# Experts in an order found on the chip: many and few tokens in turn, weights addressed by register

## The chip, the core and the metric

The kernel runs on one core of one Trainium2 chip, in one launch. The metric is the device time of that core in microseconds (us), from the first to the last instruction with what lies around it; lower is better. An expert's weights are 12 MiB of float32 (8 MiB for the gate and up projection, 4 MiB for the down projection), and all 32 experts are read from the chip's memory once: 384 MiB.

## The reference, cut to what matters

One layer of a diffusion block runs over 256 latent tokens of width 1024. Its first half (adaLN, a Fourier branch, a gated linear recurrence, a merge) is not touched by the change. Its second half is a mixture of 32 experts, of which each token takes the four with the highest router logits:

```python
logits = (t @ w_router + b_router).astype(jnp.float32)
top_v, top_i = lax.top_k(logits, TOP_K)          # 4 of 32
wts = jax.nn.softmax(top_v, axis=-1)
...
gu = xb @ w_gu[e] + b_gu[e]                      # (n, 1024) @ (1024, 2048)
gate = jnp.minimum(gu[:, :D_EXPERT], SWIGLU_LIMIT)
up = jnp.clip(gu[:, D_EXPERT:], -SWIGLU_LIMIT, SWIGLU_LIMIT)
act = (up + 1.0) * gate * jax.nn.sigmoid(SWIGLU_ALPHA * gate)
yb = act @ w_down[e] + b_down[e]                 # (n, 1024) @ (1024, 1024)
```

The result of each expert is weighted with `wts` and added into its tokens' rows; a gated residual add and a final norm follow. How many tokens an expert has depends on the data. Worked out from the reference with its inputs, the counts of experts 0 to 31 are 19, 63, 12, 15, 42, 19, 53, 12, 22, 7, 17, 49, 20, 38, 25, 54, 40, 32, 26, 81, 78, 35, 23, 65, 77, 18, 18, 35, 6, 7, 9, 7.

## The kernel before

The first half of the program, some 330 us, is written by a planner (lines 106 to 1018). It ends with the router. What matters here is the loop over the experts (line 1364).

**Weights.** SyncE issues every load of weights, in the order of the list `todo` (lines 188 to 198): gu0, gu1, dn0, gu2, dn1, gu3, dn2 and so on. `gu{e}.{k}` are the eight loads of 1 MiB of an expert's gate and up weights, `dn{e}.{k}` the four of its down weights. Every load needs one of 19 slots (`NSLOT`, line 46). `drop` gives a slot back, `pump` issues the next load into it; in the program a load then waits for the last reader of the slot that it takes. For experts 0 and 1 a slot comes free as each step k ends (line 1334). For the others all eight `gu` slots are dropped behind the conditional blocks (line 1344), and so are the four `dn` slots (line 1422). Besides, a load waits for the load eight before it to land.

**Routing.** Lines 1030 to 1050 make the logits, their mask `msk`, the place `pos` of each token in its expert's list, and the counts. `pick` and `gather` (lines 1058 and 1069) collect the rows of two experts by a matmul with a one-hot matrix. The counts are loaded into registers of TensorE, ScalarE and VectorE (line 1222); on TensorE this load stands between the first gather and the first expert.

**Experts 0 and 1** are computed with 64 rows each (`gate_up`, line 1094). **Each other expert** has room for 32 rows in one pass: `up32` (line 1111) multiplies 32 rows with all eight `gu` tiles; with more than 32 tokens a second pass runs under a condition on the count (line 1340), with more than 64 a third (line 1342). `swiglu` follows each pass. `turn` (line 1348) transposes the result, and `down` (line 1141) multiplies with the four `dn` tiles, again under the two conditions (lines 1417 and 1419; the third pass is `third_down`, line 1297). TensorE's order in an iteration e is: up of expert e + 1, a gather for the next two experts if e is even, `add_rows` (line 1283) in every fourth iteration, down of expert e, turn of expert e + 1. The experts run in the order of their index, whatever their counts are. With the counts above, experts 19, 20, 23 and 24 need three passes, experts 4, 6, 11, 13, 15, 16, 21 and 27 two, and the other 18 of the 30 one.

Of the kernel before, what the change touches and what calls it, by code (L numbers as in the profile page):

```python
# [32 lines left out]
D = 1024  # L33
# [46 lines left out]

S_C, S_CC, S_N1, S_N2, S_CW, S_CB, S_GA, S_GX, S_LAM, S_END = 0, 8, 16, 24, 32, 64, 72, 88, 104, 120

C_ID, C_UT, C_IO, C_END = 0, 128, 256, 512

B_CH, B_END = 512, 768

# [4 lines left out]
def block_kernel(ctx: ExitStack, tc: tile.TileContext, x, cx, small, b_ada, w_ada0, w_ada, w_in, gate_w,  # L91
# [84 lines left out]
    for it, j in seq:  # L176
# [8 lines left out]
        elif it[0] == "ada":  # L185
            todo.append((f"ada{8 + c}", w_ada[c // 8, c % 8], 1))

    for e in range(NE + 1):
        if e < NE:
            for k in range(KD):  # L190
                todo.append((f"gu{e}.{k}", w_gu[e * D + k * P:e * D + (k + 1) * P], 1))
        if e:
            d = e - 1
            for k in range(KD // 2):
                todo.append((f"dn{d}.{k}", w_dn[d * FE + 2 * k * P:d * FE + 2 * (k + 1) * P].rearrange(
                    "(a p) f -> p a f", p=P), 2))
            if d == 3:
                todo.append(("bd", b_dn, 0))
# [832 lines left out]
    rs2 = rstd_of(sq, 2)  # L1031
    for j in range(2):
        ada_row(ada_b[2], 2 + j, g2b[:, j * 512:(j + 1) * 512])
    pc, p = bank(), bank()
    for t in range(2):
        V.scalar_tensor_tensor(lg[:, t, :NE], pl[t][:, :NE], rs2[:, t:t + 1], lb, op0=OP.mult, op1=OP.add)
    for t in range(2):
# [6 lines left out]
    PE.matmul(p[:, :NE], lhsT=before, rhs=msk[:, 0], start=True, stop=True)  # L1044
    PE.matmul(p[:, NE:2 * NE], lhsT=before, rhs=msk[:, 1], start=True, stop=False)
    PE.matmul(p[:, NE:2 * NE], lhsT=ones, rhs=msk[:, 0], start=False, stop=True)
    for t in range(2):
        PE.matmul(pc[0:1, :NE], lhsT=ones[:, 0:1], rhs=msk[:, t], start=t == 0, stop=t == 1)
    V.scalar_tensor_tensor(pos, p[:, :2 * NE].rearrange("p (t e) -> p t e", t=2), 1.0, msk, op0=OP.add, op1=OP.mult)
    cnt = per.tile([1, NE], I32, name="cnt")  # L1050

    def col(a, t, e):
        return a[:, t, e:e + 1] if e != "x" else cols[:, (2 if a is wts else 0) + t:(2 if a is wts else 0) + t + 1]

    def pick(parts):

# [9 lines left out]
    def gather(gm, tiles):  # L1069

        n = gm.shape[-1]
        w = min(n, P)
        m = 4 if n <= P else 2
        per_tile = 512 // w
        xT = [tiles[k // per_tile][:, k % per_tile * w:(k % per_tile + 1) * w] for k in range(KD)]
        xM = [tiles[-1][:, k * CAP:(k + 1) * CAP] for k in range(KD)]
        ps = [bank() for _ in range(KD // m)]
        for k in range(KD):
            p = ps[k // m][:, k % m * n:(k % m + 1) * n]
            for t in range(2):  # L1080
                PE.matmul(p, lhsT=xs[:, t, k * P:(k + 1) * P], rhs=gm[:, t], start=t == 0, stop=t == 1)  # L1081
        for k in range(KD):
            p = ps[k // m][:, k % m * n:(k % m + 1) * n]
            for o, c in ((xT[k], slice(0, w)), (xM[k], slice(w, n)))[:1 if n <= P else 2]:
                if k % 2:
                    S.activation(o, p[:, c], AF.Identity, bias=mod2[:, 0, k:k + 1], scale=mod2[:, 1, k:k + 1])  # L1086
                else:
                    V.tensor_scalar(o, p[:, c], mod2[:, 1, k:k + 1], mod2[:, 0, k:k + 1], op0=OP.mult, op1=OP.add)  # L1088
        return xT, xM

    def one_of(e):
        return sel[:, e:e + 1] if e != "x" else selx

    def gate_up(e, ps, xT, ks):

# [110 lines left out]
    def add_start(bd):  # L1206
# [244 lines left out]
def _constants():  # L1451
    ca = np.zeros((P, C_END), np.float32)
    ca[:, C_ID:C_ID + P] = np.eye(P)
    ca[:, C_UT:C_UT + P] = np.triu(np.ones((P, P)), 1)
    ca[:, C_IO:C_IO + T] = np.arange(1, T + 1)[None, :]
    l, k = np.meshgrid(np.arange(T), np.arange(T), indexing="ij")
    th = 2 * np.pi * ((l * k) % T) / T
    dft = np.concatenate([np.cos(th)[:, :N_C], np.sin(th)[:, 1:T // 2]], 1).reshape(2, P, T).transpose(1, 0, 2)
    l, k = np.meshgrid(np.arange(P), np.arange(P), indexing="ij")
    th = 2 * np.pi * ((l * k) % P) / P  # L1460
    s = 1.0 / math.sqrt(T * P)
    cb = np.concatenate([dft.reshape(P, 2 * T), s * np.cos(th), -s * np.sin(th)], 1).astype(np.float32)
    return ca, cb
# [53 lines left out]
```

## Time and profile before

| what | value |
|---|---|
| runs, median (lowest to highest) | 1343.27 us (1332.36 to 1345.16), 3 runs |
| the profiled execution: its time | 1340.13 us |
| the profiled execution: its span | 1338.3 us, granted TensorE clock 0.905 of full |
| TensorE busy (matmul) | 1109.0 us, 83% |
| VectorE, ScalarE, GpSimd busy | 43%, 20%, 10% |
| DMA queue of SyncE | 86.1% of 16 engines over the span, 464.77 MB |

The profile shows one execution. Times in it count from the first instruction. PE stands for TensorE's matmuls, PEq, SPq and DVEq for the sequencers of TensorE, SyncE and VectorE. In the slices and windows PEclk is the granted TensorE clock as a share of full speed, and GB/s is what the core's 16 DMA engines moved. In a row of the timeline the first number is when the row starts, the second how long it lasts, xN how many instructions it holds, and the bracket how long the engine sat idle before and what ended that.

### The profile page before, as it was taken

What the parts mean: (1) busy time and instruction counts of PE and PEld (TensorE: products, weight loads), DVE (VectorE), ACT (ScalarE), POOL (GpSimd) and SP (SyncE); (2) the same over time, 40 slices, a digit from 0 to 9 for tenths busy, and PEclk for the clock granted to TensorE, in tenths of its full rate; (3) what the DMA queues carried; (4) which work ended last, traced back from release to release, by engine and by line L of the source; (5) the groups of instructions that cost most, each with busy time, mean ns of one, the idle gap of its engine ahead of it and who ended that gap; (6) DMA issues with size and microseconds to landing.
All of it is one profiled execution on the core that took longest, in us unless ns stands there. A gap on an engine that the chain in (4) does not pass through costs nothing. (4 is left out here: it accounts for less than half of the span.)

```text
span 1338.3 us, 22548 instructions
## 1 busy us (share of the span) xinstructions
PE 1109.0 (83%) x9393; PEld 619.1 (46%) x9393; DVE 574.2 (43%) x1131; ACT 270.7 (20%) x460; POOL 133.6 (10%) x125
## 2 busy tenths in 40 slices
PE   5998987889898787876878688769998988897765
PEld 4897875678444242423333243324443424443322
DVE  4469788975233332224233233323343424333222
ACT  4355686512211010101101010101010100110101
POOL 4237346600000000000000000000000000000000
PEclk8998988989998886879899899879998989998888
DMA  9920535479899999999999999999798959999994
GB/s 378 406 122 32 220 120 220 173 303 400 335 386 414 402 415 416 410 408 414 414 416 413 414 414 414 415 414 413 309 368 342 399 240 394 388 414 413 413 413 168
DMA packets 82617, 467.11 MB, mean 349 GB/s; under 512 B 8329, under 2 KB 8465, under 8 KB 42681
## 3 DMA queue, kind: packets, MB, share of 16 engines
q1 hardware_dynamic: 82457, 464.77, 86.1%
q8 instruction: 126, 2.06, 0.6%
q14 instruction: 34, 0.28, 0.1%
HBM read 463.69 MB, written 1.05 MB: 347 GB/s over the span
## 5 line engine op out<-in xcount | busy, mean ns | idle before, releaser
L1117 PE MATMUL bank<-slot,t2k 128*32 128x512 f32 x2944 | 378.8, 663 | 25.1 <-DMA slot<-in_w_gu 23.4
L1117 PEld LDWEIGHTS bank<-slot,t2k 128*32 128x32 f32 x2944 | 99.2, 120 | 273.0 <-issue 225.9
L1150 PE MATMUL bank<-slot,t2k 128*32 128x256 f32 (+1 forms) x3008 | 196.1, 406 | 14.4 <-issue 6.6
L1125 DVE TENSOR_SCALAR t2k<-bank 64x512 f32<-64x512 f32 (+1 forms) x36 | 24.6, 683 | 339.1 <-PE bank L1120 311.6
L242 PE MATMUL bank<-slot 128*128 128x256 f32 x512 | 152.0, 297 | 12.8 <-DVE slot L231 8.0
L244 PE MATMUL bank<-slot 128*128 128x256 f32 x512 | 149.5, 292 | 5.2 <-DVE slot L235 5.2
L1150 PEld LDWEIGHTS bank<-slot,t2k 128*32 128x32 f32 (+1 forms) x3008 | 107.4, 116 | 99.6 <-issue 42.6
L243 PE MATMUL bank<-slot 128*128 128x256 f32 x512 | 149.0, 291 | 0.7 <-DVE slot L235 0.7
L242 PEld LDWEIGHTS bank<-slot 128*128 128x128 f32 x512 | 102.5, 200 | 21.8 <-DVE slot L231 8.9
L244 PEld LDWEIGHTS bank<-slot 128*128 128x128 f32 x512 | 102.4, 200 | 6.0 <-DVE slot L235 6.0
L243 PEld LDWEIGHTS bank<-slot 128*128 128x128 f32 x512 | 102.4, 200 | 1.5 <-DVE slot L235 1.0
L1081 PE MATMUL bank<-gm,xs 128*128 128x192 f32 (+1 forms) x512 | 87.5, 330 | 15.0 <-PEq L1342 5.5
L1360 ACT ACTIVATE t2k<-bank 128x512 f32<-128x512 f32 x32 | 19.1, 597 | 395.7 <-PE bank L1359 395.7
L1081 PEld LDWEIGHTS bank<-gm,xs 128*128 128x128 f32 x512 | 82.9, 193 | 25.4 <-issue 22.7
L1126 ACT ACTIVATE t2k<-t2k 64x512 f32<-64x512 f32 (+1 forms) x36 | 22.7, 630 | 345.1 <-DVE t2k L1125 345.1
L1359 PE MATMUL bank<-ca,t2k 64*128 64x64 f32 (+1 forms) x128 | 17.4, 265 | 80.6 <-DVEq L1419 36.2
L1170 DVE TENSOR_TENSOR m<-bank,row 32x256 f32<-32x256 f32 x56 | 23.3, 417 | 128.1 <-PE bank L1150 127.7
L1170 DVE TENSOR_TENSOR b<-bank,row 32x256 f32<-32x256 f32 x112 | 47.3, 422 | 42.7 <-PE bank L1150 41.4
L235 DVE TENSOR_TENSOR slot<-slot 128x1024 fp32r<-128x1024 f32 (+1 forms) x40 | 54.1, 1362 | 15.8 <-ACT slot L228 12.9
L1359 PEld LDWEIGHTS bank<-ca,t2k 64*128 64x128 f32 (+1 forms) x128 | 12.5, 161 | 98.0 <-issue 56.4
L1086 ACT ACTIVATE t2k<-bank,mod 128x128 f32<-128x128 f32 x124 | 45.3, 429 | 60.4 <-DVE t2k L1088 60.2
L228 ACT ACTIVATE slot<-slot 128x1024 fp32r<-128x1024 f32 x39 | 40.6, 1054 | 58.1 <-PE bank L244 26.6
(281 smaller groups left out, 1144.7 us busy)
## 6 DMA issues: line engine op xcount, KB each, us to landing
slot<-in_w_gu SPq DMA_DIRECT2D x256, 1024.0 KB, 19.7
slot<-in_w_down SPq DMA_DIRECT2D x128, 1024.0 KB, 20.0
slot<-in_w_ada SPq DMA_DIRECT2D x24, 1024.0 KB, 8.9
slot<-in_w_in SPq DMA_DIRECT2D x18, 1024.0 KB, 10.0
slot<-in_w_rnn SPq DMA_DIRECT2D x4, 1024.0 KB, 5.6
slot<-in_w_out SPq DMA_DIRECT2D x4, 1024.0 KB, 7.9
slot<-in_gate_w SPq DMA_DIRECT2D x2, 1024.0 KB, 16.4
slot<-in_w_fourier SPq DMA_DIRECT2D x2, 1024.0 KB, 6.3
```

The source lines that it names most:

```text
L228: S.activation(hi, src, AF.Copy)
L235: V.tensor_sub(lo, src, hi)
L242: PE.matmul(p, lhsT=l[0], rhs=r[0], start=start, stop=False, skip_group_check=True)
L243: PE.matmul(p, lhsT=l[0], rhs=r[1], start=False, stop=False, skip_group_check=True)
L244: PE.matmul(p, lhsT=l[1], rhs=r[0], start=False, stop=stop, skip_group_check=True)
L1081: PE.matmul(p, lhsT=xs[:, t, k * P:(k + 1) * P], rhs=gm[:, t], start=t == 0, stop=t == 1)
L1086: S.activation(o, p[:, c], AF.Identity, bias=mod2[:, 0, k:k + 1], scale=mod2[:, 1, k:k + 1])
L1117: PE.matmul(p[j * SUB:(j + 1) * SUB], lhsT=xT[k], rhs=wt[:, j * 512:(j + 1) * 512], start=k == 0, stop=False, skip_group_check=True)
L1125: V.tensor_scalar(g, ps[0], LIMIT, None, op0=OP.min)
L1150: PE.matmul(p[h * n:(h + 1) * n, :w], lhsT=aT[:, o:o + n], rhs=wt[:, (k % 2) * D + h * w:(k % 2) * D + (h + 1) * w], start=k == 0, stop=k ...
L1170: V.tensor_mul(y[j // 2][o:o + SUB, j % 2 * 256:(j % 2 + 1) * 256], p[j * SUB:(j + 1) * SUB], g2b[j * SUB:(j + 1) * SUB, j * 256:(j + 1) * ...
L1359: PE.transpose(p[:, o:o + n], g[:, c * P:(c + 1) * P], ident[:n, :n])
```

## The change

Experts 0 and 1 stay where they are. For the other 30 the chip ranks the experts by their counts (ties by index), and a fixed table says which rank runs at which place: rank 2 (most tokens), rank 31 (fewest), rank 9, rank 24, rank 3, rank 30, rank 10, rank 23 and so on. With the counts above the passes at places 2 to 31 are 3 1 2 1, 3 1 2 1, 3 1 2 1, 3 1 2 1, 2 1 2 1, 2 1 1 1, 2 1 1 1, 1 1 (before: 1 1 2 1 2 1 1 1 1 2 1 2 1 2 2 1 1 3 3 2 1 3 3 1 1 2 1 1 1 1).

- `ordr` holds the counts by place (32 numbers) and the expert at each place (32 more). It is made from six small VectorE operations on [96, 32] and two small matmuls, behind the first gather.
- SyncE loads the expert of a place into a register (`values_load`, one for each of 30 places), and the 360 loads of those experts' weights take their address from it.
- `to_places` permutes `pos` and `wts` into `pw` by a matmul with the permutation, behind expert 0's up; `selp` does so for the bias rows. From place 2 on the code reads `pw` and `selp`.

```diff
+PAIRS = (0, 7, 1, 8, 2, 9, 3, 10, 4, 11, 5, 12, 6, 13, 14)
...
     def load(name, src, a):
         t = slot(name)
+        if callable(src):
+            src = src()
...
+    def expert(e):
+        if e < FIRST:
+            return e
+        if e not in places:
+            places[e] = nc.values_load(ordr[0:1, NE + e:NE + e + 1], engines=[ET.SP], min_val=0, max_val=NE - 1,
+                                       skip_runtime_bounds_check_because="the index of an expert by construction")
+        return places[e]
+
+    def rows_at(w, e, r, n):
+        return w[bass.ds(expert(e) * D + r, n)] if e >= FIRST else w[e * D + r:e * D + r + n]
...
-                todo.append((f"gu{e}.{k}", w_gu[e * D + k * P:e * D + (k + 1) * P], 1))
+                todo.append((f"gu{e}.{k}", lambda e=e, k=k: rows_at(w_gu, e, k * P, P), 1))
...
+    p96 = bank()
     for t in range(2):
-        PE.matmul(pc[0:1, :NE], lhsT=ones[:, 0:1], rhs=msk[:, t], start=t == 0, stop=t == 1)
+        PE.matmul(p96[:3 * NE, :NE], lhsT=ones[:, :3 * NE], rhs=msk[:, t], start=t == 0, stop=t == 1)
...
-    V.tensor_copy(cnt, pc[0:1, :NE])
...
+    V.scalar_tensor_tensor(junk, iota0[:3 * NE], 1.0, sel, op0=OP.mult, op1=OP.mult, accum_out=cc[:, 1:2])
+    V.tensor_add(key, p96[:3 * NE, :NE], ca[:3 * NE, C_TI:C_TI + NE])
+    V.scalar_tensor_tensor(junk, key, 1.0, sel, op0=OP.mult, op1=OP.mult, accum_out=cc[:, 2:3])
+    V.scalar_tensor_tensor(junk, key, cc[:, 2:3], ones[:3 * NE, :NE], op0=OP.is_gt, op1=OP.mult,
+                           accum_out=cc[:, 3:4])
+    V.tensor_scalar(pm, ca[:3 * NE, C_RK:C_RK + NE], cc[:, 3:4], None, op0=OP.is_equal)
+    V.scalar_tensor_tensor(junk, p96[:3 * NE, :NE], 1.0, sel, op0=OP.mult, op1=OP.mult, accum_out=cc[:, 0:1])
     xT, xM = gather(gm, [t2k(), t2k()])
+    pc = bank()
+    for i in (1, 0):
+        PE.matmul(pc[0:1, i * NE:(i + 1) * NE], lhsT=cc[:NE, i:i + 1], rhs=pm[:NE], start=True, stop=True)
+    V.tensor_copy(ordr, pc[0:1, :2 * NE])
+    V.tensor_scalar(selp, ca[:3 * NE, C_RK:C_RK + NE], cc[:, 3:4], None, op0=OP.is_equal)
+
+    def to_places():
+
+        p = bank()
+        for i, a in enumerate((pos, wts)):
+            for t in range(2):
+                PE.transpose(p[:NE, (2 * i + t) * P:(2 * i + t + 1) * P], a[:, t], ident)
+        q = t2k()[:NE]
+        V.tensor_copy(q, p[:NE])
+        p = bank()
+        for i in range(4):
+            PE.matmul(p[:, i * NE:(i + 1) * NE], lhsT=q[:, i * P:(i + 1) * P], rhs=pm[:NE], start=True, stop=True)
+        V.tensor_copy(pw, p[:, :4 * NE].rearrange("p (i e) -> p i e", i=4))
...
     up(0)
+    to_places()
     turn(0)
...
+    ca[:, C_RK:C_RK + NE] = np.array([0, 1] + [r for i in PAIRS for r in (2 + i, NE - 1 - i)])[None, :]
```

On SyncE's queue, before: the loads from expert 0 on, with fixed addresses.

```order
L152 DMA slot<-in_w_gu 128x2048 x16
L152 DMA slot<-in_w_down 128x2x1024 x4
L152 DMA slot<-in_w_gu 128x2048 x8
L152 DMA slot<-in_w_down 128x2x1024 x4
L152 DMA slot<-in_w_gu 128x2048 x4
```

The same place now; `cnt` is the tile of `ordr`, and the ISA rows work out an address in registers.

```order
L156 DMA slot<-in_w_gu 128x2048 x16
L156 DMA slot<-in_w_down 128x2x1024 x4
L200 TENSOR_LOAD cnt
L156 ISA
L156 DMA slot<-in_w_gu 128x2048
L156 ISA
L156 DMA slot<-in_w_gu 128x2048
```

One register load for each place from the third on, and one address instruction for each of its 12 loads, have come in; the order of the loads among themselves is the same, place for expert.

On TensorE, before: from the counts to expert 0's up.

```order
L1046 MATMUL bank<-msk,ones 128x32
L1048 MATMUL bank<-msk,ones 1x32 x2
L1081 MATMUL bank<-gm,xs 128x128 x16
L1222 TENSOR_LOAD cnt
L1100 MATMUL bank<-slot,t2k 64x512 x32
```

The same place now.

```order
L1065 MATMUL bank<-msk,ones 128x32
L1070 MATMUL bank<-msk,ones 96x32 x2
L1104 MATMUL bank<-gm,xs 128x128 x16
L1234 MATMUL bank<-t2k 1x32 x2
L1276 TENSOR_LOAD cnt
L1123 MATMUL bank<-slot,t2k 64x512 x32
```

The two matmuls that make `ordr` now stand between the gather and the register load. (Behind expert 0's bias matmuls, ahead of the transposes of its result, stand the eight matmuls of `to_places` too.)

On VectorE, before: between the first one-hot matrix and the evictions of the first gather.

```order
L1049 SCALAR_TENSOR_TENSOR pos<-bank,msk 128x64
L1064 TENSOR_SCALAR gm<-ca,pos,rs 128x64 x4
L1195 CAST cnt<-bank 1x32
L1088 TENSOR_SCALAR t2k<-bank,mod_156 128x128 x4
L1198 TENSOR_SCALAR ex<-v_3045 128x1
```

The same place now.

```order
L1087 TENSOR_SCALAR gm<-ca,pos,rs 128x64 x4
L1224 SCALAR_TENSOR_TENSOR t2k<-iota_165,sel 96x32
L1225 TENSOR_TENSOR t2k<-bank,ca 96x32
L1226 SCALAR_TENSOR_TENSOR t2k<-t2k,sel 96x32
L1227 SCALAR_TENSOR_TENSOR t2k<-t2k,ones 96x32
L1229 TENSOR_SCALAR t2k<-ca,t2k 96x32
L1230 SCALAR_TENSOR_TENSOR t2k<-bank,sel 96x32
L1111 TENSOR_SCALAR t2k<-bank,mod_156 128x128 x4
L1235 CAST cnt<-bank 1x64
L1236 TENSOR_SCALAR selp<-ca,t2k 96x32
L1252 TENSOR_SCALAR ex<-v_3045 128x1
```

The six ranking operations stand ahead of the evictions, and the copy that the register loads wait for has moved behind them.

## Rows read from the trace of the kernel before

**Rows 1.** The page's 40 equal slices of the span (33.5 us each).

```profile
PEclk8998988989998886879899899879998989998888
GB/s 378 406 122 32 220 120 220 173 303 400 335 386 414 402 415 416 410 408 414 414 416 413 414 414 414 415 414 413 309 368 342 399 240 394 388 414 413 413 413 168
```

**Rows 2.** Windows: us; busy (count) of each engine; PEclk, DMA share, GB/s.

```profile
440.00:940.00 500.00, 399.43 (x3506) 174.95 (x3502) 155.48 (x392) 47.10 (x103) 0.00 (x0) 0.88 1.02 413
940.00:1180.00 240.00, 211.13 (x2169) 97.60 (x2165) 92.62 (x223) 21.69 (x45) 0.00 (x0) 0.94 0.87 350
```

**Rows 3.** The costliest groups of the page: the passes of up32.

```profile
L1117 PE MATMUL bank<-slot,t2k 128*32 128x512 f32 x2944 | 378.8, 663 | 25.1 <-DMA slot<-in_w_gu 23.4
```

**Rows 4.** Who SyncE waited for, 920 to 1130 us: total, times, longest.

```profile
SPq L152 <- PE bank L1120: 49.5, 3, 26.3
SPq L152 <- PEq L1342: 32.0, 2, 17.4
```

**Rows 5.** Timeline of TensorE, 1075 to 1122 us: expert 24's up, expert 23's down.

```profile
1078.34 0.66 PE L1359 MATMUL bank<-ca,t2k 64*128 64x64 f32 x4 [2.64 <-DVEq L1419]
...
1080.91 9.04 PE L1117 MATMUL bank<-slot,t2k 128*32 128x512 f32 x64
...
1089.99 7.04 PE L1117 MATMUL bank<-slot,t2k 128*32 128x512 f32 x64
...
1097.08 7.04 PE L1117 MATMUL bank<-slot,t2k 128*32 128x512 f32 x64
...
1104.17 7.08 PE L1150 MATMUL bank<-slot,t2k 128*32 128x256 f32 x128
...
1114.12 3.66 PE L1150 MATMUL bank<-slot,t2k 128*32 128x256 f32 x64 [0.15 <-DVE t2k L1138]
1118.74 2.87 PE L1311 MATMUL bank<-t2k 32*128 32x512 f32 x8 [0.96 <-DVE t2k L1170]
1121.55 0.46 PE L1359 MATMUL bank<-ca,t2k 64*128 64x64 f32 x4
```

**Rows 6.** Timeline of SyncE over the same stretch: first issue, time over all.

```profile
1076.28 28.24 SPq L152 DMA_DIRECT2D slot<-in_w_gu  x5
```

**Rows 7.** Windows of 10 us: one in the later stall, one in the early one.

```profile
1095.00:1105.00 10.00, 10.00 (x108) 3.14 (x104) 3.35 (x5) 0.63 (x1) 0.00 (x0) 1.00 0.00 0
...
390.00:400.00 10.00, 9.05 (x68) 2.86 (x62) 3.17 (x5) 0.63 (x1) 0.00 (x0) 1.00 0.83 310
```

**Rows 8.** Timeline of TensorE, 355 to 395 us: the turn to experts 1 and 2.

```profile
357.52 0.81 PE L1359 MATMUL bank<-ca,t2k 128*128 128x128 f32 x4 [2.69 <-DVE t2k L1129]
...
387.06 7.07 PE L1117 MATMUL bank<-slot,t2k 128*32 128x512 f32 x64
```

**Rows 9.** Timeline of SyncE, from 380 us: the four issues ahead of expert 2's release.

```profile
381.44 14.02 SPq L152 DMA_DIRECT2D slot<-in_w_gu  x5
```

**Rows 10.** Register loads of lines 1222 and 1395: ns min/median/max, start.

```profile
L1222 PEldq TENSOR_LOAD <-cnt x1: 2317/2317/2317, 337.9 to 337.9; - x1
...
L1395 SPq TENSOR_LOAD <-more x1: 492/492/492, 554.9 to 554.9; - x1
```

**Rows 11.** Timeline of all engines, 336 to 358 us: the start of expert 0.

```profile
336.25 0.17 DVE L1195 CAST cnt<-bank 1x32 int32<-1x32 f32 x1
336.25 3.81 PE L1081 MATMUL bank<-gm,xs 128*128 128x128 f32 x32 [1.00 <-DVE gm L1064]
...
340.44 13.95 PE L1100 MATMUL bank<-slot,t2k 128*64 128x512 f32 x64 [0.38 <-issue]
...
341.04 0.41 DVE L1088 TENSOR_SCALAR t2k<-bank,mod 128x128 f32<-128x128 f32 x1 [0.53 <-ACT t2k L1086]
...
343.61 0.19 DVE L1200 SCALAR_TENSOR_TENSOR wts<-wts,msk 128x32 f32<-128x32 f32 x1 [2.10 <-ACT wts L1199]
...
354.65 0.69 DVE L1125 TENSOR_SCALAR t2k<-bank 128x512 f32<-128x512 f32 x1 [9.24 <-PE bank L1107]
```

**Rows 12.** Timeline of TensorE, 1059 to 1076 us: what two and four experts share.

```profile
1059.78 5.47 PE L1081 MATMUL bank<-gm,xs 128*128 128x192 f32 x32
...
1068.51 3.60 PE L1287 MATMUL bank<-b,ctx 128*128 128x512 f32 x8
```

More of the change, by code (lines that the diff above doesn't have):

```diff
@@ L81 @@
 S_C, S_CC, S_N1, S_N2, S_CW, S_CB, S_GA, S_GX, S_LAM, S_END = 0, 8, 16, 24, 32, 64, 72, 88, 104, 120
-C_ID, C_UT, C_IO, C_END = 0, 128, 256, 512
+C_ID, C_UT, C_IO, C_RK, C_TI, C_END = 0, 128, 256, 512, 544, 576
+PAIRS = (0, 7, 1, 8, 2, 9, 3, 10, 4, 11, 5, 12, 6, 13, 14)
 B_CH, B_END = 512, 768
@@ L186, in block_kernel @@
             todo.append((f"ada{8 + c}", w_ada[c // 8, c % 8], 1))
+    places = {}
+    ordr = None
+    def expert(e):
[7 more added lines that the diff above has]
+        return w[bass.ds(expert(e) * D + r, n)] if e >= FIRST else w[e * D + r:e * D + r + n]
     for e in range(NE + 1):
@@ L194, in block_kernel @@
             for k in range(KD // 2):
-                todo.append((f"dn{d}.{k}", w_dn[d * FE + 2 * k * P:d * FE + 2 * (k + 1) * P].rearrange(
+                todo.append((f"dn{d}.{k}", lambda d=d, k=k: rows_at(w_dn, d, 2 * k * P, 2 * P).rearrange(
                     "(a p) f -> p a f", p=P), 2))
@@ L1033, in block_kernel @@
         ada_row(ada_b[2], 2 + j, g2b[:, j * 512:(j + 1) * 512])
-    pc, p = bank(), bank()
+    p = bank()
     for t in range(2):
@@ L1046, in block_kernel @@
     PE.matmul(p[:, NE:2 * NE], lhsT=ones, rhs=msk[:, 0], start=False, stop=True)
+    V.scalar_tensor_tensor(pos, p[:, :2 * NE].rearrange("p (t e) -> p t e", t=2), 1.0, msk, op0=OP.add, op1=OP.mult)
+    ordr = per.tile([1, 2 * NE], I32, name="cnt")
+    p96 = bank()
     for t in range(2):
-        PE.matmul(pc[0:1, :NE], lhsT=ones[:, 0:1], rhs=msk[:, t], start=t == 0, stop=t == 1)
-    V.scalar_tensor_tensor(pos, p[:, :2 * NE].rearrange("p (t e) -> p t e", t=2), 1.0, msk, op0=OP.add, op1=OP.mult)
-    cnt = per.tile([1, NE], I32, name="cnt")
+        PE.matmul(p96[:3 * NE, :NE], lhsT=ones[:, :3 * NE], rhs=msk[:, t], start=t == 0, stop=t == 1)
     def col(a, t, e):
-        return a[:, t, e:e + 1] if e != "x" else cols[:, (2 if a is wts else 0) + t:(2 if a is wts else 0) + t + 1]
+        o = 2 if a is wts else 0
+        if e == "x":
+            return cols[:, o + t:o + t + 1]
+        return a[:, t, e:e + 1] if e < FIRST else pw[:, o + t, e:e + 1]
     def pick(parts):
@@ L1091, in one_of @@
     def one_of(e):
-        return sel[:, e:e + 1] if e != "x" else selx
+        return selp[:, e:e + 1] if e != "x" else selx
     def gate_up(e, ps, xT, ks):
@@ L1194, in block_kernel @@
     gm = pick([(0, 0, CAP), (1, 0, CAP)])
-    V.tensor_copy(cnt, pc[0:1, :NE])
-    xT, xM = gather(gm, [t2k(), t2k()])
+    pw = per.tile([P, 4, NE], F32, name="pw")
+    selp = per.tile([3 * NE, NE], BF, name="selp")
+    work = t2k()[:3 * NE]
+    key, pm, junk, cc = work[:, :NE], work[:, NE:2 * NE], work[:, 2 * NE:3 * NE], work[:, 3 * NE:3 * NE + 4]
+    V.scalar_tensor_tensor(junk, iota0[:3 * NE], 1.0, sel, op0=OP.mult, op1=OP.mult, accum_out=cc[:, 1:2])
[5 more added lines that the diff above has]
+    V.scalar_tensor_tensor(junk, p96[:3 * NE, :NE], 1.0, sel, op0=OP.mult, op1=OP.mult, accum_out=cc[:, 0:1])
+    xT, xM = gather(gm, [t2k(), t2k()])
+    pc = bank()
[10 more added lines that the diff above has]
+        V.tensor_copy(q, p[:NE])
+        p = bank()
+        for i in range(4):
+            PE.matmul(p[:, i * NE:(i + 1) * NE], lhsT=q[:, i * P:(i + 1) * P], rhs=pm[:NE], start=True, stop=True)
+        V.tensor_copy(pw, p[:, :4 * NE].rearrange("p (i e) -> p i e", i=4))
     for t in range(2):
@@ L1222, in block_kernel @@
     _, counts = nc.values_load_multi_w_load_instructions(
-        cnt, engines=[ET.PE, ET.Activation, ET.DVE],
+        ordr[0:1, :NE], engines=[ET.PE, ET.Activation, ET.DVE],
         skip_runtime_bounds_check_because="a count of tokens, from 0 to 256 by construction")
@@ L1455, in _constants @@
     ca[:, C_IO:C_IO + T] = np.arange(1, T + 1)[None, :]
+    ca[:, C_RK:C_RK + NE] = np.array([0, 1] + [r for i in PAIRS for r in (2 + i, NE - 1 - i)])[None, :]
+    ca[:, C_TI:C_TI + NE] = np.where(np.arange(NE) < FIRST, 4 * T * (FIRST - np.arange(NE)), -np.arange(NE) / NE)[None, :]
     l, k = np.meshgrid(np.arange(T), np.arange(T), indexing="ij")
```

## The prediction

> **What bounds the kernel now.** I read the 40 slices first. From the thirteenth slice on GB/s stands near 414 almost throughout: the loads of the experts' weights run at the rate that they can have, and the end comes when the last has landed. So a microsecond counts where the DMA engines move less than that. The slices show two such places behind the router: around the eleventh, and seven slices from 309 to 240 and back to 388 [rows 1]. The windows give the sizes: 413 GB/s over the 500 us from 440 to 940, and 350 over the 240 us from 940 to 1180 [rows 2]. Had the second stretch run at 413, its bytes would have taken 240 x 350/413 = 203.4 us, so 36.6 us are lost there.
>
> Why they are lost is read from the queue of SyncE. It waited there longest for the end of an expert's up, in one wait 26.3 us [rows 4]. Experts 19, 20, 23 and 24, of three passes each, lie in this stretch. The last of expert 24's passes ends some 23 us after the first began, and only then do its eight slots come free [rows 5]; five issues by SyncE take 28.24 us over them [rows 6], and from 1095 to 1105 nothing is moved while TensorE is busy all the time [rows 7]. The cause is therefore that TensorE has more to do there than the loads take, with 19 slots between them. That there are many such passes can be counted: 2944 records of up32 at 64 for a pass [rows 3, 5] are 46 passes, 16 more than the 30 experts need at least, as the counts say (4 experts with two more, 8 with one more).
>
> The balance per expert: 12 loads of 1.0486 MB at 413 GB/s take 30.5 us. A three-pass expert takes three passes of 7.04, its bias matmuls of 0.4, and a down side of 17.4 from 1104.17 to 1121.6 [rows 5]: 39.0 us. A one-pass expert takes 7.04 + 0.4 + 3.66 and some 3.3 for its turn with the 2.64 us wait before it [rows 5]: 14.4. A two-pass expert takes 14.1 + 0.4 + 7.1 + 3.3 = 24.9. Two experts share a gather of 5.47, four an `add_rows` of twice 3.6 [rows 12]. Experts 19 to 24, with 3, 3, 2, 1, 3 and 3 passes, three gathers and one `add_rows`, come to 219 us of TensorE against 183 us of loads: 36 us too much, which is what the window lost.
>
> **The change part by part.**
>
> (a) The stretch from 940 to 1180 loses its cause. In the new order a group of four places has 3, 1, 2 and 1 passes at most: 39.0 + 14.4 + 24.9 + 14.4 + 2 x 5.47 + 7.2 = 110.8 us of TensorE against 4 x 30.5 = 121.9 us of loads. On average TensorE keeps up, with 11 us to spare in a group. Gain: 36.6 us. It can't be more there; it could be less by what (e) says.
>
> (b) The start. No load is under way while expert 0 waits, as all 19 slots are full and expert 0's up must release the first, so what delays expert 0 delays the end. Before, TensorE's register load began at 337.9 beside the gather, took 2.32 us [rows 10], and expert 0 began at 340.44, 0.2 us behind it [rows 11]. Now that load waits for `ordr`, which VectorE copies behind the last eviction, begun at 341.04 and 0.41 long; with the copy's 0.17 [rows 11] that is 341.6, plus 2.32 and 0.2 is 344.1: 3.7 us later. The six ranking operations, at the 0.19 of a like one [rows 11] and some gaps under 2 us in all, lie beside the gather's 3.81 us of matmuls and are taken as hidden; if that cover fails they push the evictions by up to 1 us. Bounds 2 and 5.
>
> (c) `to_places`. Its four transposes lie in the 2.69 us in which TensorE waits for expert 0's swiglu [rows 8]. Then VectorE copies [32, 512], 0.69 at the price of a pass of like length [rows 11], and four small matmuls follow before the turn can start, some 0.7 with the two hand-overs. So expert 1 begins 1.4 us later again, bounds 0.7 and 2.2. The copy to `pw` and the one-hot matrices that read it are needed only after expert 1's up of 14 us.
>
> (d) Place 2 has three passes where it had one. Before, the slots of expert 2 came free behind its one pass at 387.06 + 7.07 + 0.4; SyncE had got out four loads from 381.44 on while expert 0's down freed their slots, and the fifth issue waited [rows 9]. That cost 10 x (1 - 310/413) = 2.5 us between 390 and 400 [rows 7], so the loads were already run dry there. Now the release comes two passes of 7.04 later, and 1.4 us later from (c), while the loads ahead of it have only moved by the 3.7 of (b). Nothing else can be loaded meanwhile: 15.5 us more are lost. It is the same event as at expert 24, where a window of 10 us moved nothing. Bounds: 10, if a part of the lead is left that the early window hides, and 19, if its passes run like the 9.04 one [rows 5].
>
> (e) Later stalls. After (d) the loads are again ahead of TensorE by all the slots. A group gives back 11 us of that lead, so the next three-pass expert, four places on, would lose 14.1 - 11 = 3 us, the one after nothing; the two-pass expert between them and waits that my balance leaves out (the transposes of `comb`, the leftover table at place 3) may cost as much again. I take 7, bounds 0 and 28 (both following three-pass experts like place 2).
>
> [...] The trace shows the clock at 0.6 to 0.9 in slices where TensorE waits for loads, and near 1.0 where it is driven [rows 1]; expert 24's first pass, after waits of 2.64 and 1.3 us, took 9.04 us and the next 7.04 [rows 5]. [...] What this would cost here is rival 2, worked out from rows.
>
> (f) SyncE. 30 register loads, 0.49 us each [rows 10], and 360 address instructions. A load of weights passes every 30.5/12 = 2.54 us, and eight may be under way, so up to about 2 us more per issue is covered. I take 0. The trace shows no register-addressed load; bounds 0 and, if each cost 2.32 [rows 10] with an issue of 0.4 (an estimate: the rest of the 28.24 us and of [rows 9] is waiting), (2.72 - 2.54) x 360 = 65. The nearest row is the 0.49.
>
> Sum: -36.6 + 3.7 + 1.4 + 14.1 + 7 + 0 = -10.4 us (the 1.4 and 14.1 are the 15.5 of (d)). The profiled execution took 1340.13, so 1329.7; it lies 3.1 below the median of the runs, 1343.27. Against the median: **1333**.
>
> **Rivals.**
>
> 1. Full gain. Place 2's long up doesn't starve the loads, because TensorE works off the full slots during experts 0 and 1 and the loads keep a lead to live on. For it: the early stall was only 2.5 us [rows 7]. Against: it was there with one pass already. Then -36.6 + 5.1 = -31.5: 1312.
>
> 2. Slower: TensorE becomes the bound at places 2 to 17. If each of a group's seven up passes started slow like the 9.04 one, 14 us come on top of 110.8, and with some 3 us for `comb` and other waits that the balance leaves out a group takes 128 against 121.9: 6 too much. It decides from the point where a group passes 121.9, that is with four slow passes of seven. Then no lead is given back. At worst the two stalls of (e) come in full and four groups add 6 each: -36.6 + 19.2 + 28 + 24 = +35; halfway between that and the forecast's -10.4 is +12: 1355. Against: the second pass was at full speed [rows 5], and where TensorE is behind it doesn't idle.
>
> 3. Register addressing throttles the loads, the end of (f): 1333 + 65 = 1398, or a part of it. Against: SyncE's spare time.
>
> 4. The order on the chip doesn't separate the heavy experts (a wrong rank). Then the stalls of 36.6 come back wherever they meet, plus the added 19: 1343 + 19 = 1362. The ranking by count with ties by index speaks against it.
>
> **How the numbers follow.** Forecast 0.62 (own range 1322 to 1344), rival 1 0.17, rival 2 0.13, rivals 3 and 4 0.04 each. The range leaves out rivals 3 and 4 and the far halves of 1 and 2: 1307 to 1355. About 1%, 13.4 us, is what a measurement of this kernel can tell from no change; that is 1329.8 and 1356.7. Of the forecast 0.3 lies below 1329.8, 0.19, with rival 1 0.36. Slower: half of rival 2, and most of 3 and 4, 0.12. The same: 0.52.
>
> **What would show it.** Right: no window between 440 and 1300 far under 413 except behind the first one or two three-pass places; a gap of about 17 us with nothing moved at some 398 to 415; expert 0 starting at about 344. The step (d) is wrong if that gap is under 8 us; (a) if a stretch of 240 us at 350 is still there; (b) if expert 0 starts before 342; rival 2 if gaps come back at each fourth place up to 17; rival 3 if GB/s is lower throughout while SyncE is never waiting.

## The result and the profile after

The kernel after takes **1352.68 us** (median of 20 runs, 1348.20 to 1358.08), the kernel before, run beside it, 1337.38 (20 runs, 1332.36 to 1351.26). The ratio is 1.0089, with an interval of 1.0069 to 1.0109: some 12 us slower, where 10 us faster were forecast. The profiled span grew from 1338.3 to 1354.6 us.

The slices of after, to be read beside [rows 1]:

```profile
PEclk8998987989899979698988999989989897878868
GB/s 381 410 105 32 218 148 187 191 332 378 252 369 259 410 411 413 337 356 256 416 416 417 360 416 415 393 415 415 415 415 416 417 415 415 415 415 415 415 411 127
```

The seven poor slices behind the twenty-eighth are gone; new ones stand at the thirteenth and from the seventeenth to the nineteenth. Windows over the same stretches size them (us; busy and count of PE, PEld, DVE, ACT, POOL; granted clock, DMA share, GB/s), of before:

```profile
335.00:350.00 15.00, 13.62 (x83) 7.73 (x84) 4.27 (x20) 5.13 (x9) 0.00 (x0) 1.00 0.62 233
350.00:390.00 40.00, 37.31 (x194) 15.95 (x194) 11.90 (x30) 5.35 (x12) 0.00 (x0) 0.96 1.02 418
390.00:430.00 40.00, 35.37 (x278) 16.38 (x274) 15.07 (x39) 5.36 (x12) 0.00 (x0) 0.95 0.97 390
...
540.00:700.00 160.00, 127.46 (x1148) 58.65 (x1140) 49.08 (x122) 16.08 (x36) 0.00 (x0) 0.89 1.01 412
```

and of after, where the last row answers to the second of [rows 2]:

```profile
335.00:350.00 15.00, 10.50 (x60) 6.29 (x62) 4.86 (x29) 3.75 (x7) 0.00 (x0) 0.89 0.29 97
350.00:390.00 40.00, 35.93 (x171) 17.27 (x169) 10.95 (x28) 5.77 (x12) 0.00 (x0) 0.91 0.93 375
390.00:430.00 40.00, 40.00 (x318) 12.95 (x318) 14.59 (x31) 3.35 (x6) 0.00 (x0) 1.00 0.62 251
...
540.00:700.00 160.00, 137.71 (x1188) 57.76 (x1190) 54.85 (x134) 13.82 (x29) 0.00 (x0) 0.86 0.87 352
700.00:940.00 240.00, 205.35 (x2016) 94.93 (x2012) 88.11 (x216) 24.89 (x53) 0.00 (x0) 0.93 0.99 405
940.00:1180.00 240.00, 184.32 (x1696) 88.62 (x1692) 74.96 (x188) 23.74 (x51) 0.00 (x0) 0.89 1.02 415
```

Read each row as load time lost against 414 GB/s: its length times (1 - GB/s / 414). The stretch from 940 to 1180 lost 37.1 us before and nothing now. The others lose more than before: 4.9 (335 to 350), 4.2 (350 to 390), 13.4 (390 to 430), 23.2 (540 to 700) and 5.2 (700 to 940, which lost nothing before). That makes 50.9 lost for 37.7 won, +13 us, where the ratio says +12. These two executions differ by 16.3 us in their spans; the other 3 us lie behind 1180 us, at the end, and were not traced.

Further lines of after answer to rows shown of before. The passes of up32 are as many as in [rows 3]: the work is the same, only its order is not.

```profile
L1140 PE MATMUL bank<-slot,t2k 128*32 128x512 f32 x2944 | 375.0, 662 | 20.2 <-DMA slot<-in_w_gu 20.2
```

And where SyncE had waited up to 26.3 us for the end of an up [rows 4], from 920 to 1130 us its longest waits are now for its own transfers, 3.6 us at most but for one of 6.6:

```profile
SPq L156 <- DMA slot<-in_w_down: 53.3, 26, 3.6
SPq L156 <- DMA slot<-in_w_gu: 48.9, 35, 2.0
SPq L156 <- PEq L1396: 10.3, 2, 6.6
```

**The start.** TensorE's timeline of after, to be read beside [rows 8, 11] (start, us over all, instruction; in brackets the idle time before and its releaser):

```profile
335.55 3.81 PE L1104 MATMUL bank<-gm,xs 128*128 128x128 f32 x32 [0.86 <-DVE gm L1087]
339.29 0.27 PE L1234 MATMUL bank<-t2k 32*1 32x32 f32 x4
343.51 15.65 PE L1123 MATMUL bank<-slot,t2k 128*64 128x512 f32 x64 [3.94 <-DVE ex L1255]
...
364.20 1.91 PE L1248 MATMUL bank<-t2k 32*128 32x32 f32 x8 [4.07 <-DVE t2k L1245]
...
367.09 15.81 PE L1123 MATMUL bank<-slot,t2k 128*64 128x512 f32 x64
...
396.26 4.07 PE L1140 MATMUL bank<-slot,t2k 128*32 128x512 f32 x36
```

TensorE's register load of the counts, and expert 1's up in the kernel before:

```profile
L1276 PEldq TENSOR_LOAD <-cnt x1: 2327/2327/2327, 341.0 to 341.0; - x1
...
358.26 15.44 PE L1100 MATMUL bank<-slot,t2k 128*64 128x512 f32 x64
```

Expert 0's up starts 3.1 us later than before (340.44) and takes 15.65 instead of 13.95, behind an idle time of 3.94 us instead of 0.38. The register load, from 341.0 to 343.3, ends 0.2 us ahead of this up (the bracket names another releaser, as the profile doesn't count this load as busy); e8 shows that it is what the up waits for. Expert 1 starts at 367.09 instead of 358.26: 3.1 us from the later start, 1.7 from the longer up, and another 4.1 (so place 2's up starts at 396.26 instead of 387.06). Part of the 4.1 is on ScalarE: the load of the activation table for expert 0's swiglu. It lay beside expert 0's up before (at 346.60) and now stands on the path behind it:

```profile
360.18 1.28 ACT L1149 ACT_TABLE_LOAD   x1 [16.12 <-DVE t2k L1148]
```

**Place 2.** SyncE issues a load at 395.78, and its next one waits for place 2's up; the two take 22.12 us:

```profile
395.78 22.12 SPq L156 DMA_DIRECT2D slot<-in_w_gu  x2
```

while the window shows TensorE busy throughout at a clock of 1.00 and hardly a byte moving, as at expert 24 before [rows 7]:

```profile
404.00:418.00 14.00, 14.00 (x134) 4.21 (x126) 5.31 (x9) 1.26 (x2) 0.00 (x0) 1.00 0.01 3
```

**Place 6**, for which the prediction had 3 us, from an average balance. TensorE in after:

```profile
518.46 7.07 PE L1140 MATMUL bank<-slot,t2k 128*32 128x512 f32 x64
...
532.65 7.05 PE L1140 MATMUL bank<-slot,t2k 128*32 128x512 f32 x64
...
544.64 1.81 PE L1271 MATMUL bank<-slot,t2k 32*128 32x512 f32 x2 [4.39 <-DVE t2k L1267]
546.37 2.08 PE L1273 MATMUL bank<-xs,ca 128*128 128x512 f32 x2
...
561.25 4.00 PE L1173 MATMUL bank<-slot,t2k 128*32 128x256 f32 x64
...
568.26 8.77 PE L1140 MATMUL bank<-slot,t2k 128*32 128x512 f32 x64
```

Behind the three passes of place 6's up and ahead of place 5's down stands `add_start`, called at `e == 5`: it adds the experts' down biases and starts the sum. It waits 4.39 us for VectorE's copy of its transposed weights and then holds TensorE with 16 matmuls, eight pairs of 2.07, until some 560.5. The windows around it:

```profile
540.00:561.00 21.00, 16.61 (x22) 4.68 (x20) 4.42 (x7) 0.63 (x1) 0.00 (x0) 0.62 1.02 405
561.00:570.00 9.00, 6.60 (x86) 3.03 (x88) 4.93 (x18) 0.60 (x1) 0.00 (x0) 0.88 0.36 134
...
600.00:630.00 30.00, 28.37 (x281) 10.91 (x280) 8.92 (x19) 1.86 (x3) 0.00 (x0) 0.89 0.47 182
```

The loads live on the eight slots that place 6's up has freed. The next slot in line holds the table of down biases, which `add_start` reads (line 1271), and SyncE waits for that in one piece. Its waits for `add_start`'s matmuls in after (400 to 700 us) and, at line 1217, in before (335 to 1180 us):

```profile
SPq L156 <- PE bank L1271: 13.1, 1, 13.1
...
SPq L152 <- PE bank L1217: 0.2, 1, 0.2
```

So the loads run dry from 561 on, and again from 600 to 630, as TensorE is behind. In the kernel before the same step lay behind an expert of two passes, with the loads at 416 GB/s beside it:

```profile
505.00:526.00 21.00, 16.54 (x20) 4.61 (x19) 4.21 (x6) 0.63 (x1) 0.00 (x0) 0.57 1.01 416
```

### The profile page after: what moved, and what is told of

The parts are those of the page before. It is cut to its first block, busy times and chain, and to the rows that moved or that the text cites. A ratio compares the mean times of both kernels' runs of the same rounds, so it can differ in the third digit from the quotient of the medians.

```text
span 1354.6 us, 23332 instructions
## 1 busy us (share of the span) xinstructions
PE 1116.7 (82%) x9409; PEld 625.6 (46%) x9409; DVE 577.1 (43%) x1144; ACT 271.7 (20%) x460; POOL 133.6 (10%) x125
## 5 line engine op out<-in xcount | busy, mean ns | idle before, releaser
L1140 PE MATMUL bank<-slot,t2k 128*32 128x512 f32 x2944 | 375.0, 662 | 20.2 <-DMA slot<-in_w_gu 20.2
L1173 PEld LDWEIGHTS bank<-slot,t2k 128*32 128x32 f32 (+1 forms) x3008 | 103.4, 115 | 98.7 <-issue 39.3
L1104 PE MATMUL bank<-gm,xs 128*128 128x192 f32 (+1 forms) x512 | 98.6, 355 | 34.6 <-PEq L1396 22.3
L1104 PEld LDWEIGHTS bank<-gm,xs 128*128 128x128 f32 x512 | 93.0, 212 | 47.3 <-issue 39.4
L1111 DVE TENSOR_SCALAR t2k<-bank,mod 128x128 f32<-128x128 f32 x124 | 40.8, 373 | 58.1 <-PE bank L1104 45.3
```

What stands on the lines that cost most here:

```text
L1140: PE.matmul(p[j * SUB:(j + 1) * SUB], lhsT=xT[k], rhs=wt[:, j * 512:(j + 1) * 512], start=k == 0, stop=False, skip_group_check=True)
L1173: PE.matmul(p[h * n:(h + 1) * n, :w], lhsT=aT[:, o:o + n], rhs=wt[:, (k % 2) * D + h * w:(k % 2) * D + (h + 1) * w], start=k == 0, stop=k ...
```

## The experiments

Theory A: the loads stand where TensorE's work between two releases outlasts what the 19 slots hold, and three places do that now: the start, place 2's three passes, and place 6's three passes with `add_start` behind them. The rivals were that the new instructions themselves slow the loads (register addressing), that the passes alone cost at place 6, and that all stalls share one lead, so that one taken away comes back at the next. Each ratio is against the kernel before run on the same chip; microseconds are the ratio's share of 1338 (1% is 13.4).

A difference between two ratios carries some 4 to 6 us of doubt from their intervals.

GB/s of each kernel's profile by stretch, read from windows like those above. Each is one execution: from 390 to 430, which the edit of e7 doesn't touch, it has 365 where before has 390, that is 2.4 us.

| kernel | ratio, interval | 335-350 | 350-390 | 390-430 | 430-540 | 540-700 | 700-940 | 940-1180 |
|---|---|---|---|---|---|---|---|---|
| before | 1 | 233 | 418 | 390 | 411 | 412 | 414 | 350 |
| after | 1.0089 (1.0069-1.0109) | 97 | 375 | 251 | 412 | 352 | 405 | 415 |
| e1_index_order | 1.0091 (1.0058-1.0123) | 79 | 376 | 383 | 412 | 414 | 414 | 341 |
| e2_fixed_order | 1.0058 (1.0036-1.0080) | 217 | 418 | 309 | 393 | 358 | 407 | 414 |
| e3_bias_late | 0.9991 (0.9970-1.0012) | 90 | 381 | 248 | 412 | 396 | 405 | 409 |
| e4_start_both | 1.0006 (0.9983-1.0029) | 282 | 399 | 312 | 393 | 360 | 411 | 415 |
| e5_all | 0.9781 (0.9747-0.9815) | 227 | 419 | 394 | 396 | 408 | 405 | 414 |
| e6_swap | 0.9955 (0.9934-0.9977) | 86 | 374 | 390 | 400 | 375 | 414 | 415 |
| e7_before_bias20 | 1.0088 (1.0048-1.0128) | 251 | 417 | 365 | 413 | 414 | 411 | 334 |
| e8_counts_late | 1.0033 (1.0008-1.0058) | 235 | 383 | 249 | 411 | 361 | 410 | 415 |

**e1_index_order**: all that the change adds, but the ranks are the indices, so the order is that of before.

```diff
-    ca[:, C_RK:C_RK + NE] = np.array([0, 1] + [r for i in PAIRS for r in (2 + i, NE - 1 - i)])[None, :]
+    ca[:, C_RK:C_RK + NE] = np.arange(NE)[None, :]
-    ca[:, C_TI:C_TI + NE] = np.where(np.arange(NE) < FIRST, ...)
+    ca[:, C_TI:C_TI + NE] = -4 * T * np.arange(NE)[None, :]
```

> All of the change's instructions, but the ranking key is minus the index, so the experts run in the order of before. Theory A (the new instructions cost at the start only): the loads lose about 9 us more than before between 335 and 390 us, nothing more anywhere, and the stretch of 350 GB/s around experts 19 to 24 is still there: before + 9, bounds + 6 and + 12. Rival R (register-addressed loads are slower one by one): GB/s in the 500 us ahead of expert 19 is under 410 instead of 413, and the time is over before + 15.

Measured: 1352.17 us, before + 12. From 430 to 940 us its rates are those of before (412, 414, 414), though every load from the third place on is addressed by register: the addressing costs nothing there. The start loses 12.1 us at 335 to 350 and 3.7 at 350 to 390, some 9.6 more than before. The rest is in the old cluster, where it loses 5.2 us more than before:

```profile
940.00:1180.00 240.00, 210.28 (x2112) 93.85 (x2116) 87.16 (x209) 21.09 (x44) 0.00 (x0) 0.92 0.85 341
```

Its loads there run some 10 us later, but this isn't the window's edge: from 940 to 1200 e1 moves 343 GB/s and before 355, which makes 7.5 us. The clock over these 260 us is 0.91 in e1 and 0.94 in before; why was not tried. So "nothing more anywhere" was wrong.

**e2_fixed_order**: the kernel before with this input's order written in as constants, and none of the change's instructions.

```diff
+PLACE = (0, 1, 19, 28, 4, 3, 20, 31, 16, 10, 24, 29, 13, 26, 23, 9, 21, 25, 15, 30, 27, 5, 6, 7, 17, 12, 11, 2, 18, 8, 14, 22)
...
-                todo.append((f"gu{e}.{k}", w_gu[e * D + k * P:e * D + (k + 1) * P], 1))
+                todo.append((f"gu{e}.{k}", w_gu[PLACE[e] * D + k * P:PLACE[e] * D + (k + 1) * P], 1))
```

(and the same at `w_dn`, `col`, `one_of` and `counts`).

> The new order alone, written into the program as 32 constants, with none of the change's instructions. Theory A: the 37 us around experts 19 to 24 are gained, place 2 costs some 13 and the places from 6 on some 24 to 28: before + 0 to + 4, that is about 9 to 12 us under the changed kernel. Rival R: 20 us or more under before, since all the loss would have come with the register addresses.

Measured: 1346.78, before + 8, more than was expected. The order alone wins the 37 us and loses as many again between 390 and 940, most of it at places 2 and 6. The end, which neither theory had, adds to it. Its last two pieces of TensorE's work,

```profile
1322.88 5.35 PE L1151 MATMUL bank<-slot,t2k 128*32 128x256 f32 x64 [0.17 <-ACTq L1264]
1330.12 5.40 PE L1289 MATMUL bank<-b,ct 128*128 128x512 f32 x8 [1.90 <-DVEq L1419]
```

took 3.66 and 3.70 in the kernel before, where the first began at 1319.00: 3.9 us of the 7.3 between the two spans come from the later start, 3.4 from these two being slower, with no loads left to wait for, in windows with a clock of 0.69 and 0.77 where before has 1.00. Why they start later was not traced.

The two halves, 12 us in e1 and 8 in e2, come to more than the 12 of the whole. The extra loss in e1's cluster has no place in the new order, and after has a slow end only in part (5.34 and 3.70 us for the like pieces).

**e3_bias_late**: after, with `add_start` and the load of its table moved from place 5 to place 21.

```diff
-            if d == 3:
+            if d == 19:
...
-        if e == 5:
+        if e == 21:
             add_start(held["bd"][:NE, :D])
```

> The changed kernel with the bias and residual matmuls (add_start) moved from place 5 to place 21, and the load of b_down with them. Theory A (they meet the three-pass expert of place 6): the 24 us that the loads lose between 540 and 700 us fall to 6 or less, and the time to the changed kernel - 18, that is before - 3; bounds - 12 and - 24. Rival 2 of the prediction (TensorE too slow at places 2 to 17 by the order itself, with slow first passes): less than 6 us change, the gaps behind place 6 stay.

Measured: 1338.05, after - 13. The stretch of places 6 and 7 went from 352 to 396 GB/s, from 24.0 us lost to 7.0 (6 or less were expected), while place 2's (248) stayed:

```profile
540.00:700.00 160.00, 137.38 (x1258) 62.31 (x1250) 56.33 (x141) 16.75 (x37) 0.00 (x0) 0.90 0.97 396
```

So it isn't the three passes alone: `add_start` makes most of the stall. (The slot of its table moves with it, so this run doesn't part the two.) At place 21, in the order of pairs, it takes the same 2.07 a pair, and the stretch around it still moves 409.

**e4_start_both**: after, with the counts' register loads behind expert 1's up (nothing reads them sooner), and `to_places` in two halves between expert 0's matmuls.

```diff
-    _, counts = nc.values_load_multi_w_load_instructions(ordr[0:1, :NE], ...)
+    counts = None
...
+                if e == 0 and k == 4:
+                    q = to_places()
+                if e == 0 and k == 6:
+                    to_places_end(q)
...
     up(0)
-    to_places()
...
+        if e == 0:
+            _, counts = nc.values_load_multi_w_load_instructions(ordr[0:1, :NE], ...)
```

> The changed kernel with the register loads of the counts moved behind expert 1's up, and to_places cut in two parts that run among expert 0's matmuls. Theory A: expert 0's first matmul follows the gather by 1 us, and expert 1 begins some 8 us earlier against the gather than in the changed kernel; the start's 9 us come back nearly whole: the changed kernel - 7, bounds - 4 and - 9. Rival S (the place-2 stall swallows what the start gives): less than 2 us change, as the loads run dry at the same time.

Measured: 1339.52, after - 11 by the ratios, more than expected. (Later expectations go by the medians, 13.2 for this run and 14.6 for e3.) The start (335 to 390) now loses 6.2 us, as before the change, and place 2's stretch also gained (251 to 312), where its up now begins at 384.38 instead of 396.26. Part came back at once: 430 to 540 lost 5 us more.

**e8_counts_late**: the first half of e4 alone (the register loads moved, `to_places` left behind expert 0's up).

> The kernel after with nothing but the counts' register loads moved behind expert 1's up; to_places stays behind expert 0's up. Theory A (the start's loss is mostly TensorE waiting 3.9 us for the counts and then working slowly behind the wait): after - 6 to after - 10 us, with the loss of 335 to 350 us down from 11 to about 5. Rival (to_places between up and turn costs more than its own 1.9 us of matmuls, through the table load and the copy that it waits for): after - 1 to after - 4 us, the rest of e4's 13.2 being to_places.

Measured: 1341.88, after - 7.5. By the medians the wait for the counts is the larger half, as expected; the 3.6 us that e4 has beyond this run are within the noise. TensorE's timeline splits the two:

```profile
339.70 13.95 PE L1123 MATMUL bank<-slot,t2k 128*64 128x512 f32 x64
...
358.70 1.91 PE L1248 MATMUL bank<-t2k 32*128 32x32 f32 x8 [4.07 <-DVE t2k L1245]
...
361.58 15.28 PE L1123 MATMUL bank<-slot,t2k 128*64 128x512 f32 x64
```

Expert 0's up follows the gather without a wait and is at 13.95 again; expert 1's, behind the 4.07 us wait of `to_places`, still takes 15.28. That much isn't new: in the kernel before it took 15.44, behind 2.69 us of idling [rows 8].

**e6_swap**: after, with each pair turned round, few tokens first.

```diff
-    ca[:, C_RK:C_RK + NE] = np.array([0, 1] + [r for i in PAIRS for r in (2 + i, NE - 1 - i)])[None, :]
+    ca[:, C_RK:C_RK + NE] = np.array([0, 1] + [r for i in PAIRS for r in (NE - 1 - i, 2 + i)])[None, :]
```

> The kernel after with nothing but each pair turned round: few tokens, then many. Places 2, 4, 6 hold few, 3, 5, 7 many, and add_start of place 5 stands behind place 6's up of one pass. Theory A (the loss of 390 to 430 us comes from three passes at place 2 before TensorE has a lead, that of 540 to 630 us from add_start directly behind three passes): both become small, the start's 9 stays: after - 13 to after - 22 us, before - 7 to before + 3. Rival B (the loss is the number of passes among places 2 to 7, whichever comes first): after - 4 to after + 4 us.

Measured: 1332.77, after - 18, before - 6. The start is as slow as in after (86 GB/s), yet place 2's stretch is whole again:

```profile
390.00:430.00 40.00, 39.27 (x306) 12.75 (x308) 14.35 (x32) 4.00 (x8) 0.00 (x0) 1.00 0.97 390
...
540.00:700.00 160.00, 144.12 (x1427) 68.08 (x1426) 61.61 (x149) 15.50 (x33) 0.00 (x0) 0.95 0.92 375
```

The number of heavy experts among places 2 to 7 is the same, so it is which comes first that counts. From 540 to 700 still 15 us are lost; in e5, where `add_start` is gone from there too, 2.3.

**e7_before_bias20**: the kernel before with `add_start` at place 20, in its cluster of heavy experts.

```diff
-            if d == 3:
+            if d == 18:
...
-        if e == 5:
+        if e == 20:
             add_start(held["bd"][:NE, :D])
```

> The kernel before with add_start moved from place 5 to place 20, into its own cluster of experts of many tokens. Theory A (the 21 us of add_start on TensorE are paid wherever TensorE has no slack): before + 12 to before + 22 us, and the loss stands between 940 and 1180 us. Rival (add_start costs little by itself; what cost at place 6 of the kernel after is the three passes alone): before - 3 to before + 4 us.

Measured: 1354.62, by the ratio before + 12 (6 to 17), at the lower end of Theory A; the rival is out. The stretch from 940 to 1180 fell from 350 to 334 GB/s, 9.3 us more lost. It is less than the 21 us that I put in, for a reason the trace shows: here `add_start` takes 1.12 a pair and not 2.07, and with its wait 11 us, at a clock of 1.00.

```profile
998.65 1.12 PE L1217 MATMUL bank<-slot,t2k 32*128 32x512 f32 x2 [1.99 <-DVE t2k L1213]
```

```profile
996.00:1007.00 11.00, 9.01 (x21) 2.67 (x19) 2.12 (x4) 1.53 (x5) 0.00 (x0) 1.00 1.02 411
```

So what the loads lose is close to the time that `add_start` holds TensorE, where TensorE has no slack: 9.3 of 11 us here, and 17 of 21 between after and e3.

**e5_all**: after with the edits of e3, e4 and e6 together.

```diff
-            if d == 3:
+            if d == 19:
...
-    to_places()
...
-        if e == 5:
+        if e == 21:
...
-    ca[:, C_RK:C_RK + NE] = np.array([0, 1] + [r for i in PAIRS for r in (2 + i, NE - 1 - i)])[None, :]
+    ca[:, C_RK:C_RK + NE] = np.array([0, 1] + [r for i in PAIRS for r in (NE - 1 - i, 2 + i)])[None, :]
```

> The kernel after with three edits: the counts' register loads behind expert 1's up and to_places inside expert 0's up (as in e4), the bias's add_start at place 21 (as in e3), and each pair of places as few tokens, then many. Theory A (each stretch loses load time by its own cause, so the savings add, and the stretch of places 18 to 22 keeps its gain of 37 us): e3's 14.6 and e4's 13.2 off the kernel after, and some 5 to 8 more since place 2 now holds few tokens: before - 15 to before - 22 us, 1315 to 1322. Rival B (one store of lead: a stall taken away in one stretch returns in the next, so the edits overlap): no better than e3 or e4 alone, before + 1 to before - 5 us.

Measured: **1310.43 us**, ratio 0.9781 (0.9747 to 0.9815): 29 us faster than before and 41 faster than after, better than I expected and the best of all kernels here. The three edits won 13, 11 and 18 us alone, 42 in sum. So rival B (one store of lead) is out at this size. The totals add, but by stretch the edits overlap, so that is in part luck: from 540 to 700 e3, e4 and e6 win 17.0, 3.1 and 8.9 us of load time, and e5 21.7; from 390 to 430 e4 and e6 win 5.8 and 13.4, and e5 13.8. Expert 0 starts behind the gather, the table load lies beside it, and expert 1's up is at full speed, which it wasn't in before (15.44):

```profile
339.68 8.80 PE L1123 MATMUL bank<-slot,t2k 128*64 128x512 f32 x40
344.26 1.28 ACT L1149 ACT_TABLE_LOAD   x1
359.19 13.96 PE L1123 MATMUL bank<-slot,t2k 128*64 128x512 f32 x64
```

```profile
390.00:430.00 40.00, 39.27 (x320) 16.16 (x313) 17.85 (x39) 5.16 (x11) 0.00 (x0) 1.00 0.98 394
...
540.00:700.00 160.00, 141.89 (x1342) 64.97 (x1338) 56.23 (x135) 17.16 (x38) 0.00 (x0) 0.96 1.00 408
...
940.00:1180.00 240.00, 192.29 (x1662) 86.15 (x1654) 76.52 (x190) 22.83 (x50) 0.00 (x0) 0.88 1.02 414
```

Against before it keeps the 37 us and pays back some 11, from 430 to 540 (4.8 lost), 540 to 700 (2.3) and 700 to 940 (5.2).

## Why the prediction was wrong

The gain was right; what was given back was some 23 us more than the sum had. By its steps:

- **(a)**, the stretch from 940 to 1180: -36.6 forecast, -37.7 read. e2, e4, e5 and e6 have it too (414 or 415 GB/s), with or without the new instructions, so it is the order's.
- **(b)**, the start: +3.7 for a later expert 0, and it started 3.1 later (344.1 forecast, 343.51 read), the wait for `ordr` being where it was put. What failed is the price of what follows: the up behind that wait took 1.7 us more. The windows show the clock at 0.81 and then at 1.00, while TensorE was busy all the time in both:

```profile
344.00:352.00 8.00, 8.00 (x32) 2.99 (x30) 0.61 (x4) 0.06 (x1) 0.00 (x0) 0.81 0.48 165
352.00:360.00 8.00, 8.00 (x42) 3.18 (x38) 0.59 (x1) 0.00 (x0) 0.00 (x0) 1.00 1.01 426
```

  The prediction had seen one pass slower behind waits (9.04 against 7.04 at expert 24, [rows 5]) and used it only for rival 2, at the heavy places. At the start the traces show the like: 15.65 behind 3.94 us of idling in after, 13.95 behind none in e8, where the clock is 1.00 from 339.7 to 353.7. Behind 2.69 us expert 1's up went either way: 15.44 in before, 13.96 in e5.
- **(c)**, `to_places`: +1.4 forecast, 4.1 read. The four transposes went into the gap as said, but the gap grew, as the table load of 1.28 fell into it, and the matmuls behind it took 1.91 where 0.7 was put in (1.07 in e4, in the middle of expert 0's up). In e5, with both halves inside expert 0's up, they lie hidden. Both parts of the start together: 9.1 us of loads instead of 5.1. e4 shows 11 us to be had there and e8 7.5 for the counts alone; what is left for `to_places`, 3.6, is within the noise.
- **(d)**, place 2: 14.1 forecast and 13.4 read, by the mechanism named, a gap from 404 to 418 with TensorE driven. e6 takes it away by putting an expert of few tokens there.
- **(e)**, later stalls, is the step that failed: +7 forecast, +28 read (23.2 from 540 to 700, 5.2 from 700 to 940). The prediction gave a group 11 us of slack from a balance of ups, downs, gathers and `add_rows`. It named two things that the balance leaves out (the transposes of `comb`, the leftover table) and missed a dearer third: `add_start`, 21 us of TensorE once, in the group with place 6. It was in the trace before, from 505 to 526, where it cost nothing because TensorE had slack there; with the heavy expert in front of it SyncE waited 13.1 us for it instead of 0.2, and it cost most of its length: 17 of the 28 us are gone in e3. e3 (moved away: -13 us) and e7 (put beside heavy experts in the kernel before: +12) show it two ways; e6 (a light expert ahead of it) fits. The bound of 28 held the size, but for another reason: not two heavy places like place 2, but one place with another long step behind it. What is left in e3, 7.0 us from 540 to 700 and 5.2 from 700 to 940, is 12 where (e) had 7. Part of that may be a second miss of the balance, which put every pass at 7.04: in after the first pass of each place from 7 to 15 took 8.4 to 9.6 us (8.77 at 568.26). What those cost was not tried.
- **(f)**, register addressing: 0 forecast, and nothing found. In e1 the rates from 430 to 940 are 412 to 414; the 30 register loads took 0.27 us each (median) in after:

```profile
L200 SPq TENSOR_LOAD <-cnt x30: 262/273/483, 347.6 to 1272.9; - x30
```

Of the rivals, the first (full gain) is refuted by place 2. The second asked for gaps at each fourth place up to 17; the slices are full again from the twentieth on but for two, so TensorE did not become the bound on average. Its condition did come about, as at places 7 to 15 the first pass of each place, four of a group's seven, was slow; the time came near its 1355 by another way, with `add_start` in the largest part, and that is luck. The third and fourth are refuted by e1 and by (a).

With the measured terms in place of the forecast ones the sum is -37.7 + 9.1 + 13.4 + 28.1 = +13 (28.1 with the 0.3 won from 430 to 540), against +12 by the ratio.

## What to carry to other kernels

When a change reorders work, lay the one-off steps (a bias, a table, a start of sums) on the new order too, one by one from the timeline: a step that is free in a stretch with slack can cost most of its length behind a heavy one. An average balance by group hides this; what counts is the work between two releases of the buffers against what the buffers hold. And begin an order of heavy and light with a light one, since at the start there is no lead to live on, and put a new wait behind work that doesn't need it (no condition before place 2's up at 396 reads the counts that TensorE waited for until 343).

## What the runs showed of the hardware

- The eight pairs of `add_start` ran at 2.07 us each (the first one in after at 1.81) in before, after, e3 and e5, in windows with a clock of 0.57, 0.62, 0.57 and 0.53, though TensorE was busy there for more than 16 of 21 us; they had idled 4.46, 4.39, 4.63 and 4.23 us just ahead. From 510 to 526 in before and from 545 to 561 in after the clock is 0.50, with TensorE busy for all of the 16 us. In e7, behind 1.99 us of idling, they ran at 1.12 with the clock at 1.00. That the clock stayed low through 16 us of matmuls I had not expected; why it did was not tried.
- An activation table's load of 1.28 us stands on the path in after (360.18) and in e8 (354.68), and beside expert 0's up in before (346.60) and e5 (344.26). It goes with `to_places` standing behind that up, not with the wait for the counts; why was not tried.
- At the end of the kernel, where the loads are over, the last two pieces of TensorE's work took 7.36 us in before, at a clock of 1.00, and 10.75 in e2, in windows of 0.69 and 0.77: 3.4 us more. In after the like pieces took 5.34, in a window of 0.72 (1332 to 1338), and 3.70.
